# Order of the state-space products on TensorE: neighbours in different quarters of the array's columns

## The chip, the cores and the metric

The kernel runs on one core of a Trainium2 chip. The metric is the device time of one execution in microseconds, the median over several runs. The kernel before took 517.58 us (three runs, 512.52 to 519.69 us).

## What is computed

An encoder trunk of two layers over 256 tokens of 1024 channels, in float32. Each layer normalises its input, projects it into three branches, and projects the gated branches back. The first branch is a bidirectional state-space model: 32 groups of 16 channels drive a complex diagonal state of 64 numbers each.

```python
for l in range(DEPTH):
    h = rmsnorm(x, norm_g[l])
    xa, za, qb, kb, vb, zb, qc, kc, vc, zc = jnp.split(h @ w_in[l], split_points, axis=-1)
    ya = ssm_branch(xa, ...) * silu(za)       # state-space branch
    yb = na_branch(qb, kb, vb, ...) * silu(zb)       # neighbourhood attention, 8 heads
    yc = dilated_branch(qc, kc, vc, ...) * silu(zc)  # dilated attention, 8 heads
    x = x + concatenate([ya, yb, yc]) @ w_out[l]
return rmsnorm(x, final_g)

# ssm_branch, per direction: bu = b_bar u;  h = scan(lam_bar, bu);  y += Re(c h)
# then g = gelu(y), out = g * sigmoid(g @ glu_w + glu_b)
```

## The kernel before

The work of all stages is written as generators, each of which yields the engine and the buffers that its next step needs. A planner (`Flow.run`) with its own cost for each operation picks the next step by the earliest start and a rank, and so fixes, when the kernel is built, one order of instructions for each engine. `in_order` keeps that order. The planner's cost of a product depends on its shape and not on its neighbours. All weight and scratch transfers are issued by SyncE's queue (SP), in the planner's order too.

The big projections (`run_layer`, tile `pj`) take weights in pieces of 512 KB (`raw`). A piece is split into a high part `whi` (cast, ScalarE or VectorE) and a low part `wlo` (subtraction on VectorE), and TensorE forms three products. There are three buffers of `raw` and `whi` and two of `wlo`, so transfers, splitting and products move on together.

The state-space branch runs in chunks of T = 8 tokens, with four batches (`b`) of eight groups (`GB`) in each layer:

- `ssm_x` multiplies the chunked input `u` with the tables `wb` into the bank `psx`, and transposes into `E`, the chunk states.
- `ssm_scan` runs the recurrence over chunks on VectorE (`t1s`, `t2s`, `E`).
- `ssm_out` forms the tables `wc` on VectorE, two halves of four groups for each batch.
- `ssm_kernels` multiplies `bd` and `bs` (ScalarE copies) with `wc` and `cc` into the bank `psr`. Copies `rs`, by ScalarE and then VectorE, go through device memory (`rd`) and come back as `toep`, eight transfers for each batch.
- `ssm_y` copies `E` to `hy`, and adds three products per group in the bank `psy`: `u` with `toep`, and the two parts of `hy` with `wc`. The result goes on as `yt`, `ys`, `yd`, `yT` to the gate of the branch.

In `psx`, `psr` and `psy` the product of a group has 32 output rows, so it uses a quarter of the array's columns: `tile_position=(0, 32 * g4)` for group `g4` of a half `h`, with output in the 32 partitions from `32 * g4`. `psr` and `psy` take all products of a group in turn, and then the next group. `psx` has one product per group, and so goes from quarter to quarter. In a half, `psr` has for each group two products of T * CH = 128 columns and two of CH = 16 columns; `psy` has three of 128 columns.

Of the kernel before, what the change touches and what calls it, by code (L numbers as in the profile page):

```python
# [20 lines left out]
P = 128  # L21
# [8 lines left out]
CH = 16  # L30
T = 8
# [72 lines left out]
def ap(base, offset, dims):  # L104
    return bass.AP(base.tensor, base.offset + offset, dims)
# [8 lines left out]
class Event:  # L114
    t, eng = None, None
# [223 lines left out]
def trunk(ctx: ExitStack, tc: tile.TileContext, io):  # L339
    nc = tc.nc  # L340
    flow = Flow(tc)
    V, A, G, PE, SP = flow.V, flow.A, flow.G, flow.PE, flow.SP
# [5 lines left out]
    def new(tag, dims, dtype=F32, name=None):  # L348

        return sb.tile([P] + dims, dtype, name=name or tag, tag=tag, bufs=SLOTS[tag])  # L350

    def bank(tag, name=None):
        return psum.tile([P, 512], F32, name=name or tag, tag=tag, bufs=SLOTS[tag])

    def one(name, dims, dtype=F32, bufs=1):
        return sb.tile([P] + dims, dtype, name=name, tag=name, bufs=bufs)

    def dma(out, src):
        SP.dma_start(out, src)

    def copy(eng, out, src):
        if eng == "V":
            V.tensor_copy(out, src)
        else:
            A.copy(out, src)
# [45 lines left out]
    bd = one("bd", [2, GB, CH, 2])  # L411
# [50 lines left out]
    class Piece:  # L462
# [6 lines left out]
        def free(self):  # L469
            flow.free(*(("raw",) if self.plain else ("whi", "wlo")))  # L470
# [400 lines left out]
    def ssm_out(L, tb):  # L871

        for b in range(NB):
            wcs = []
            for h in range(2):
                g0 = b * GB + 4 * h
                yield "V", "g4", "tm", tb.ev, tb.wb_ev[2 * NB - 1]
                wc = new("g4", [2, 4, T, CH], name="wc")

                def qbc(t, i):  # L880
                    return free(t, i * T * GROUPS + g0, [[1, 4], [GROUPS, T], [0, CH]])

                def cbc(t, i):
                    return free(t, (i * GROUPS + g0) * CH, [[CH, 4], [0, T], [1, CH]])

                tm = new("tm", [4, T, CH], name="tmo")
                V.tensor_mul(tm, cbc(tb.csum, 0), qbc(tb.qc, 0))
                yield "V"
                V.tensor_mul(wc[:, 0], cbc(tb.cc, 1), qbc(tb.qsd, 0))
                yield "V"  # L890
                V.tensor_mul(wc[:, 1], cbc(tb.cc, 0), qbc(tb.qsd, 1))
                yield "V"
                V.tensor_sub(wc, free(tm, 0, [[0, 2], [1, 4 * T * CH]]), wc)
                flow.free("tm")
                wcs.append(wc)
            tb.wc.append(wcs)
            flow.set(tb.wc_ev[b])
            flow.spawn(ssm_kernels(L, b, tb, wcs), L.l)
            if b == NB - 1:
                flow.set(tb.wcs_ev)  # L900

    def ssm_kernels(L, b, tb, wcs):
        bb = tb.bb
        yield "A", "bd", "bs"
        bs = new("bs", [2, GB, CH, 2])
        for ri in range(2):
            src = free(bb, (ri * GROUPS + b * GB) * CH, [[1, GB * CH], [0, 2]])
            (A.copy if ri == 0 else lambda o, i: A.mul(o, i, -1.0))(bs[:, ri], src)
            yield "A"
        for d in range(2):  # L910
            r = slice(d * NST, (d + 1) * NST)
            A.copy(bd[r, :, :, :, d], bs[r, :, :, :, d])
            if d == 0:
                yield "A"
        yield "PE", "sm"
        ps = bank("sm", "psr")
        n = (T + 1) * CH
        for h in range(2):
            for g4 in range(4):
                g = 4 * h + g4  # L920
                o = ps[32 * g4:32 * g4 + 32, h * n:(h + 1) * n]
                for ri in range(2):
                    PE.matmul(o[:, :T * CH], lhsT=bd[:, ri, g].rearrange("p c d -> p (c d)"),
                              rhs=wcs[h][:, ri, g4].rearrange("p t c -> p (t c)"),
                              start=(h == 0 and ri == 0), stop=ri == 1, skip_group_check=True,
                              tile_position=(0, 32 * g4))
                for ri in range(2):
                    PE.matmul(o[:, T * CH:], lhsT=bs[:, ri, g].rearrange("p c d -> p (c d)"),
                              rhs=tb.cc[:, ri, b * GB + g], start=False, stop=ri == 1,
                              skip_group_check=True, tile_position=(0, 32 * g4))  # L930
        flow.free("bd", "bs")
        yield "A", "rs"
        rs = new("rs", [2, T + 1, CH])
        for h in range(2):
            A.copy(rs[:, h, :T, :], ps[:, h * n:h * n + T * CH].rearrange("p (t c) -> p t c", t=T))
        yield "V"
        for h in range(2):
            V.scalar_tensor_tensor(rs[:, h, T, :], eye16, tb.dsk[:, 2 * b + h:2 * b + h + 1],
                                   ps[:, h * n + T * CH:(h + 1) * n], ALU.mult, ALU.add)
        flow.free("sm")  # L940
        if b == NB - 1:
            flow.free("tab")
        yield "SP"
        rd = dram.tile([2, 4, CH, 15, CH], F32, name="rd", bufs=4)
        rdv = rd.rearrange("h g c t e -> (g c) h t e")
        dma(rdv[:, :, 0:7, :], rs[1::2, :, 1:T, :])
        dma(rdv[:, :, 7, :], rs[0::2, :, T, :])
        dma(rdv[:, :, 8:15, :], rs[0::2, :, 0:T - 1, :])
        flow.free("rs")
        flow.settle()  # L950

        tag = "toep" if b < TOEP else "qkv"
        yield ("SP", tag) if b < TOEP else ("SP", tag, L.br[1].v_ev[1])
        toep = new(tag, [GB, T * CH], name="toep")
        for g in range(GB):
            dma(toep[:, g, :], ap(rd, g * 15 * CH * CH, [[15 * CH, CH], [CH, T], [1, T * CH]]))
            if g % 2 and g < GB - 1:
                yield "SP"
        tb.toep[b] = toep
        flow.set(tb.toep_ev[b])  # L960

    def ssm_y(L, b, tb):
        gs = slice(b * GB, (b + 1) * GB)
        eng = yield "A/V", tb.scan_ev, tb.toep_ev[b], "hy"
        E = tb.E
        hy = new("hy", [2, GB, NCH])
        copy(eng, hy[:NST], E[:NST, :, gs, :NCH])
        eng = yield "A/V"
        copy(eng, hy[NST:], free(E[NST:], b * GB * N1 + NCH - 1, [[RS, 2], [N1, GB], [-1, NCH]]))
        yield "PE", "sm"  # L970
        wcs, u, toep = tb.wc[b], L.u[b], tb.toep[b]
        py = bank("sm", "psy")
        for h in range(2):
            for g4 in range(4):
                g = 4 * h + g4
                o = py[32 * g4:32 * g4 + 32, h * P:(h + 1) * P]
                PE.matmul(o, lhsT=u[:, g, :], rhs=toep[:, g, :], start=h == 0, stop=False,
                          skip_group_check=True, tile_position=(0, 32 * g4))
                for ri in range(2):
                    PE.matmul(o, lhsT=hy[:, ri, g, :], rhs=wcs[h][:, ri, g4].rearrange("p t c -> p (t c)"),  # L980
                              start=False, stop=ri == 1, skip_group_check=True, tile_position=(0, 32 * g4))
        flow.free("toep" if b < TOEP else "qkv", "g4", "g4", "u", "hy")
        tb.y_left -= 1
        if tb.y_left == 0:
            flow.free("E")
        yield "A", "yt"
        yt = new("yt", [2, P])
        A.copy(yt, py[:, :256].rearrange("p (h d) -> p h d", h=2))
        flow.free("sm")
        yield "PE", "sm"  # L990
        py2 = bank("sm", "psy2")
        for h in range(2):
            PE.transpose(py2[:, h * P:(h + 1) * P], yt[:, h, :], ident)
        flow.free("yt")
        yield "A", "ys"
        ys = new("ys", [GB, NCH])
        A.copy(ys, py2[:, :256].rearrange("p (g k) -> p g k", g=GB))
        flow.free("sm")
        yield "SP", L.yT.ask()
        yd = dram.tile([T, P, NCH], F32, name="yd")  # L1000
        dma(ap(yd, 0, [[S, P], [1, S]]), ys)
        flow.free("ys")
        flow.settle()
        yield "SP"
        dma(L.yT.tile[:, b, :].rearrange("p (t k) -> p t k", t=T), yd.rearrange("t c k -> c t k"))
        flow.set(L.y_ev[b])
# [665 lines left out]
```

## Time and profile before

| | |
|---|---|
| median of three runs | 517.58 us (512.52 to 519.69) |
| the profiled execution | 511.08 us, its span 509.3 us |
| busy share of the span: TensorE, weight loads, VectorE, ScalarE, GpSimd | 95%, 86%, 75%, 58%, 5% |
| granted TensorE clock, mean | 0.981 |
| mean share of the transfer engines' time, main queue | 70.1% |

A float32 product stands as two pairs of a weight load (PEld) and a product (PE) in the trace. The time of a product there is from its entry to its modelled end, so consecutive products overlap; the step from one start to the next is what it costs. Times are from the span's start.

### The profile page before, as it was taken

What the parts mean: (1) busy time and instruction counts of PE and PEld (TensorE: products, weight loads), DVE (VectorE), ACT (ScalarE), POOL (GpSimd) and SP (SyncE); (2) the same over time, 40 slices, a digit from 0 to 9 for tenths busy, and PEclk for the clock granted to TensorE, in tenths of its full rate; (3) what the DMA queues carried; (4) which work ended last, traced back from release to release, by engine and by line L of the source; (5) the groups of instructions that cost most, each with busy time, mean ns of one, the idle gap of its engine ahead of it and who ended that gap; (6) DMA issues with size and microseconds to landing.
All of it is one profiled execution on the core that took longest, in us unless ns stands there. A gap on an engine that the chain in (4) does not pass through costs nothing.

```text
span 509.3 us, 10599 instructions
## 1 busy us (share of the span) xinstructions
PE 483.6 (95%) x4076; PEld 436.0 (86%) x4076; DVE 381.3 (75%) x745; ACT 297.0 (58%) x596; POOL 24.6 (5%) x45
## 2 busy tenths in 40 slices
PE   8887988999999999989999699999999999999995
PEld 7676786698888999989998599998989799999995
DVE  5966767988997895457879678889788994358533
ACT  6432366566587665455545436767676776587432
POOL 1000102110000000000000010222000000000000
PEclk9988999999999999999999889999999999999999
DMA  7987798865663779874767997877565585664512
GB/s 261 299 236 247 218 258 232 222 172 166 140 143 106 219 260 278 245 215 162 252 205 211 262 268 204 186 170 178 136 126 134 138 261 182 184 167 168 187 41 84
DMA packets 73331, 99.61 MB, mean 196 GB/s; under 512 B 26768, under 2 KB 48400, under 8 KB 73280
## 3 DMA queue, kind: packets, MB, share of 16 engines
q1 hardware_dynamic: 73136, 98.83, 70.1%
q8 instruction: 32, 0.52, 0.4%
q14 instruction: 19, 0.16, 0.1%
q10 hardware_dynamic: 144, 0.10, 0.1%
HBM read 93.19 MB, written 5.72 MB: 194 GB/s over the span
## 4 chain that ended last, share of the span: by engine, by line
PE 67%; DMA 20%; DVE 6%; SPq 2%; ACT 2%; issue 2%; POOL 0%; DVEq 0%; POOLq 0%; ACTq 0%
PE pj L135 45%; PE psr L135 6%; PE sc L135 5%; DMA raw<-w_in 4%; DMA wb<-b_c 3%; DMA u<-xad 3%; PE po L135 3%; PE pp L135 3%; PE psy L135 3%; SPq L135 2%; DVE wb L135 2%; PE psx L135 2%; DMA qd<-qbt 2%; DMA raw<-w_out 1%; DMA xad<-xa 1%
## 5 line engine op out<-in xcount | busy, mean ns | idle before, releaser
L135 DVE TENSOR_TENSOR wlo<-raw,whi 128x1024 fp32r<-128x1024 f32 x92 | 113.6, 1234 | 55.6 <-PE pj L135 28.6
L135 ACT CAST whi<-raw 128x1024 fp32r<-128x1024 f32 x91 | 95.0, 1048 | 67.3 <-DMA raw<-w_in 28.2
L135 PE MATMUL pj<-h0h,whi 128*128 128x256 f32 x192 | 58.3, 304 | 0.0
L135 PE MATMUL pj<-h1h,whi 128*128 128x256 f32 x192 | 56.3, 293 | 0.0
L135 PE MATMUL pj<-h0h,wlo 128*128 128x256 f32 x192 | 55.1, 287 | 0.7 <-DVE wlo L135 0.7
L135 PE MATMUL pj<-h0l,whi 128*128 128x256 f32 x192 | 54.9, 286 | 0.0
L135 PE MATMUL pj<-h1h,wlo 128*128 128x256 f32 x192 | 53.9, 281 | 0.0
L135 PE MATMUL pj<-h1l,whi 128*128 128x256 f32 x192 | 53.9, 281 | 0.0
L135 PEld LDWEIGHTS pj<-h0h,whi 128*128 128x128 f32 x192 | 37.4, 195 | 5.7 <-issue 5.5
L135 PEld LDWEIGHTS pj<-h1h,whi 128*128 128x128 f32 x192 | 36.3, 189 | 2.7 <-issue 2.7
L135 PEld LDWEIGHTS pj<-h0h,wlo 128*128 128x128 f32 x192 | 37.3, 194 | 1.0 <-DVE wlo L135 0.9
L135 PEld LDWEIGHTS pj<-h0l,whi 128*128 128x128 f32 x192 | 37.3, 194 | 0.0
L135 PEld LDWEIGHTS pj<-h1h,wlo 128*128 128x128 f32 x192 | 36.2, 189 | 0.0
L135 PEld LDWEIGHTS pj<-h1l,whi 128*128 128x128 f32 x192 | 36.1, 188 | 0.0
L135 PE MATMUL pj<-xin,raw 128*128 128x256 f32 x128 | 32.5, 404 | 3.6 <-DMA raw<-w_in 2.8
L135 ACT ACTIVATE pt<-pt,sm 128x160 f32<-128x160 f32 (+1 forms) x63 | 28.3, 469 | 10.5 <-DVE sm L135 10.2
L135 PEld LDWEIGHTS pj<-xin,raw 128*128 128x128 f32 x128 | 24.5, 200 | 10.2 <-DVE xin L135 3.0
L135 PE MATMUL sc<-k,q 64*128 64x256 f32 (+1 forms) x128 | 31.0, 362 | 2.1 <-DVE nm L135 2.1
L135 ACT ACTIVATE pt<-pt,nm 128x160 f32<-128x160 f32 (+1 forms) x64 | 29.8, 468 | 5.3 <-DVE nm L135 5.1
L135 PE MATMUL psr<-wc,bd 128*32 128x128 f32 x256 | 31.1, 279 | 0.0
L135 POOL TENSOR_TENSOR bias<-bias,namask 128x320 f32<-128x320 f32 x16 | 19.5, 1220 | 222.8 <-DMA bias<-rpb 99.9
L135 PEld LDWEIGHTS sc<-k,q 64*128 64x128 f32 x128 | 19.8, 186 | 9.9 <-DVE nm L135 3.6
(198 smaller groups left out, 1300.5 us busy)
## 6 DMA issues: line engine op xcount, KB each, us to landing
raw<-w_in SPq DMA_DIRECT2D x78, 512.0 KB, 4.6
raw<-w_out SPq DMA_DIRECT2D x24, 512.0 KB, 3.4
wb<-b_c SPq DMA_DIRECT2D x32, 256.0 KB, 7.7
qrp<-qd SPq DMA_DIRECT2D x32, 256.0 KB, 5.0
bias<-vdram SPq DMA_DIRECT2D x16, 256.0 KB, 4.9
toep<-rd SPq DMA_DIRECT2D x64, 64.0 KB, 3.9
bias<-rpb SPq DMA_DIRECT2D x32, 116.0 KB, 5.5
raw<-glu_w SPq DMA_DIRECT2D x4, 512.0 KB, 4.0
```

The costliest lines, as they stand in the source:

```text
L135: return f(*args, **kw)
```

## The change

Two loops are turned inside out. In `ssm_kernels`, for each half, the first products of all four groups come first, then the second products of all four, and the same for the short products. In `ssm_y`, for each half, `u` with `toep` for four groups, then the first part of `hy` with `wc` for four groups, then the second. Operands, targets, number of products and the accumulation in each group's target stay.

```diff
@@ -915,17 +915,20 @@
         yield "PE", "sm"
         ps = bank("sm", "psr")
         n = (T + 1) * CH
+
         for h in range(2):
-            for g4 in range(4):
-                g = 4 * h + g4
-                o = ps[32 * g4:32 * g4 + 32, h * n:(h + 1) * n]
-                for ri in range(2):
-                    PE.matmul(o[:, :T * CH], lhsT=bd[:, ri, g].rearrange("p c d -> p (c d)"),
+            for ri in range(2):
+                for g4 in range(4):
+                    PE.matmul(ps[32 * g4:32 * g4 + 32, h * n:h * n + T * CH],
+                              lhsT=bd[:, ri, 4 * h + g4].rearrange("p c d -> p (c d)"),
                               rhs=wcs[h][:, ri, g4].rearrange("p t c -> p (t c)"),
                               start=(h == 0 and ri == 0), stop=ri == 1, skip_group_check=True,
                               tile_position=(0, 32 * g4))
-                for ri in range(2):
-                    PE.matmul(o[:, T * CH:], lhsT=bs[:, ri, g].rearrange("p c d -> p (c d)"),
+            for ri in range(2):
+                for g4 in range(4):
+                    g = 4 * h + g4
+                    PE.matmul(ps[32 * g4:32 * g4 + 32, h * n + T * CH:(h + 1) * n],
+                              lhsT=bs[:, ri, g].rearrange("p c d -> p (c d)"),
                               rhs=tb.cc[:, ri, b * GB + g], start=False, stop=ri == 1,
                               skip_group_check=True, tile_position=(0, 32 * g4))
         flow.free("bd", "bs")
@@ -971,14 +974,14 @@
         wcs, u, toep = tb.wc[b], L.u[b], tb.toep[b]
         py = bank("sm", "psy")
         for h in range(2):
-            for g4 in range(4):
-                g = 4 * h + g4
-                o = py[32 * g4:32 * g4 + 32, h * P:(h + 1) * P]
-                PE.matmul(o, lhsT=u[:, g, :], rhs=toep[:, g, :], start=h == 0, stop=False,
-                          skip_group_check=True, tile_position=(0, 32 * g4))
-                for ri in range(2):
-                    PE.matmul(o, lhsT=hy[:, ri, g, :], rhs=wcs[h][:, ri, g4].rearrange("p t c -> p (t c)"),
-                              start=False, stop=ri == 1, skip_group_check=True, tile_position=(0, 32 * g4))
+            for part in range(3):
+                for g4 in range(4):
+                    g = 4 * h + g4
+                    PE.matmul(py[32 * g4:32 * g4 + 32, h * P:(h + 1) * P],
+                              lhsT=u[:, g, :] if part == 0 else hy[:, part - 1, g, :],
+                              rhs=toep[:, g, :] if part == 0 else wcs[h][:, part - 1, g4].rearrange("p t c -> p (t c)"),
+                              start=h == 0 and part == 0, stop=part == 2, skip_group_check=True,
+                              tile_position=(0, 32 * g4))
         flow.free("toep" if b < TOEP else "qkv", "g4", "g4", "u", "hy")
         tb.y_left -= 1
         if tb.y_left == 0:
```

## Rows read from the trace of the kernel before

**Rows 1.** The page, the chain that ended last: shares of the span by line.
```profile
PE pj L135 45%; PE psr L135 6%; PE sc L135 5%; DMA raw<-w_in 4%; DMA wb<-b_c 3%; DMA u<-xad 3%; PE po L135 3%; PE pp L135 3%; PE psy L135 3%; SPq L135 2%; DVE wb L135 2%; PE psx L135 2%; DMA qd<-qbt 2%; DMA raw<-w_out 1%; DMA xad<-xa 1%
```
**Rows 2.** Busy time by stretch: start:end, us, busy us (instructions), granted clock, DMA share, GB/s.
```profile
105.00:176.00 71.00, 71.00 (x674) 62.78 (x674) 62.05 (x130) 48.85 (x113) 0.00 (x0) 1.00 0.60 157
176.00:226.00 50.00, 47.74 (x501) 45.35 (x497) 32.06 (x55) 25.14 (x40) 0.22 (x1) 1.00 0.85 246
...
324.60:388.00 63.40, 63.40 (x624) 56.13 (x623) 54.12 (x103) 42.25 (x107) 7.54 (x11) 1.00 0.71 158
...
423.40:446.00 22.60, 22.60 (x294) 21.41 (x294) 6.89 (x7) 11.57 (x21) 0.00 (x0) 1.00 0.65 181
```
**Rows 3.** Tile `psr`: ns min/median/max; first stage's stretch; its TensorE timeline (start, us).
```profile
L135 PE MATMUL psr<-wc,bd x256: 272/273/297, 105.1 to 387.2; 128*32 128x128 f32 x128
...
L135 PE MATMUL psr<-cc,bs x256: 179/183/183, 105.5 to 387.4; 128*32 128x16 f32 x128
...
105.06:109.01 3.95, 3.94 (x64) 3.90 (x64) 0.00 (x0) 0.00 (x0) 1.00 0.95 179
...
105.53 0.30 PE L135 MATMUL psr<-wc,bd 128*32 128x128 f32 x1
105.56 0.25 PE L135 MATMUL psr<-cc,bs 128*32 128x16 f32 x3
105.67 0.49 PE L135 MATMUL psr<-wc,bd 128*32 128x128 f32 x3
...
106.00 0.30 PE L135 MATMUL psr<-wc,bd 128*32 128x128 f32 x1
```
**Rows 4.** Tile `psy`, layer 1's first stage: its stretch, and its TensorE timeline.
```profile
423.38:425.90 2.52, 2.51 (x48) 2.31 (x48) 0.00 (x0) 1.00 0.84 255
...
423.63 0.27 PE L135 MATMUL psy<-wc,hy 128*32 128x128 f32 x1
423.64 0.30 PE L135 MATMUL psy<-toep,u 128*32 128x128 f32 x1
423.74 0.27 PE L135 MATMUL psy<-wc,hy 128*32 128x128 f32 x1
```
**Rows 5.** Tile `psx`, a half batch and a whole batch: busy PE, PEld, ACT.
```profile
98.37:98.95 0.58, 0.58 (x8) 0.16 (x8) 0.00 (x0) 1.00 0.99 396
278.47:279.48 1.01, 1.00 (x16) 0.42 (x16) 0.00 (x0) 1.00 0.57 109
...
L135 PEld LDWEIGHTS psx<-wb,u x128: 106/109/155, 58.0 to 369.6; 128*32 128x32 f32 x128
```
**Rows 6.** Waits (us in total, times, longest), 105 to 176, 324.6 to 388; VectorE's timeline.
```profile
DVE rs L135 <- ACT rs L135: 5.7, 4, 1.8
...
DVE rs L135 <- ACT rs L135: 5.5, 3, 2.0
...
388.23 0.42 DVE L135 CUSTOM_DVE_ANT_0 pt<-sc,bias 128x256 f32<-128x256 f32 x1 [1.24 <-PE pp L135]
```
**Rows 7.** Chain that ended last, 170 to 230 us: shares by line; pieces (start, us).
```profile
by line: DMA raw<-w_out 12.7%; SPq L135 12.5%; PE pj L135 11.5%; DMA toep<-rd 11.4%; DMA yd<-ys 9.0%; DMA yT<-yd 8.1%; DMA raw<-w_in 7.4%; PE psr L135 6.6%; PE psy L135 4.3%; issue 2.7%; ACT L135 2.1%; ACT hy L135 1.9%; DVE wlo L135 1.9%; A
...
175.96 0.37 DVE rs L135 x2
176.33 0.93 DVE t2s L135
```
**Rows 8.** Timelines: VectorE's second `wc` of layer 0, ScalarE's `hy` of layer 1.
```profile
100.15 1.22 DVE L135 TENSOR_TENSOR wc<-tmo,wc 128x1024 f32<-128x1024 f32 x1
...
422.21 0.63 ACT L135 COPY hy<-E 64x512 f32<-64x512 f32 x1
```
**Rows 9.** Stretches around a half clock, all work; last row `psx` alone. Clock third from last.
```profile
287.60:291.60 4.00, 0.00 (x0) 0.00 (x1) 3.30 (x4) 0.71 (x1) 0.50 (x1) 0.63 1.10 275
...
288.70:295.50 6.80, 3.87 (x21) 3.10 (x22) 3.16 (x4) 1.32 (x2) 0.00 (x0) 0.50 1.05 259
...
291.60:292.64 1.04, 1.01 (x8) 0.23 (x8) 0.00 (x0) 0.50 1.06 271
```

## The prediction

> **What bounds the kernel now.** I read the chain that ended last first. TensorE's big projections `pj` carry 45% of it; the chunk kernels `psr` are 6% of the span and the chunk outputs `psy` 3% [rows 1]. Then the busy time by stretch [rows 2]. From 105 to 176 us (layer 0) and from 324.6 to 388 us (layer 1), which hold four `psr` stages each, TensorE has no idle time, but VectorE has little: 71.00 − 62.05 = 8.95 us and 63.40 − 54.12 = 9.28 us. A gain of TensorE there runs into VectorE soon. From 176 to 226 us TensorE is 95% busy, yet the chain runs through VectorE, SyncE's queue and transfers [rows 7]; a gain of TensorE in that stretch is mostly turned into waiting. From 423.4 to 446 us (the four `psy` stages of layer 1) TensorE has no idle time and VectorE works 6.89 of 22.60 us: there TensorE alone sets the pace.
>
> **The present order, one stage.** A float32 product stands in the trace as two instructions, so a `psr` stage has 64 and a `psy` stage 48. In `psr`, eight instructions of one group write the same quarter before the next quarter's turn. Three of 128 columns last 0.49 us together, one alone 0.273 us: a step of (0.49 − 0.27)/2 = 0.109 us. Three of 16 columns last 0.25 us, one alone 0.183 us: a step of 0.03 us. A new group begins every 106.00 − 105.53 = 0.47 us [rows 3]: four steps of 0.109 us, with only the short products of the last group beside the next one's first. So the stage is serial, 8 × 0.47 us plus its end, and takes 3.93 us; all eight do. In `psy` the next group begins earlier: the first product of the second group starts at 423.64 us, between the third instruction (423.63) and the fourth (423.74) of the first, with three of that group still to start [rows 4]. The same holds in `psr`: the next group starts with the fifth of eight. I read both as a short queue in front of each quarter: what is listed next goes ahead as soon as no more than three instructions wait for the quarter before it. The stage then takes 2.51 us.
>
> **What the change costs.** It adds, removes and moves no instruction to another engine or queue; it permutes products within a stage, and the planner's cost for a stage is the same sum, so I take the order on every engine, the DMA issues too, as unchanged outside the stages. `psx` already has the wanted order, two instructions a quarter and then the next quarter. Sixteen of 256 columns take 1.00 us, eight take 0.58 us [rows 5]. Eight more cost 0.43 us, which is two steps of 0.215 us: four quarters run in the time of one. A stage is then two steps per eight instructions and 0.58 − 0.43 = 0.15 us of beginning and end.
> - `psr` after: a quarter has, in each half, four instructions of 0.109 us and four of 0.03 us. 2 × (0.436 + 0.12) + 0.15 = 1.26 us against 3.93 us: 2.67 us a stage, 21.4 us over eight.
> - `psy` after: 2 × 6 × 0.109 + 0.15 = 1.46 us against 2.51 us: 1.05 us a stage, 4.2 us over the four of layer 1, 4.2 us over those of layer 0.
> - New waits: the second half's `wc` is wanted some 1.3 us sooner in a stage. In the first stage it was ready at 100.15 + 1.22 = 101.37 us [rows 8] for a stage that starts at 105.06 us, so nothing waits. In `psy` four `toep` products now stand ahead of the first that reads `hy`, a small gain where `hy` comes last.
>
> The cost of a short product in four quarters at once is shown nowhere. Below lies zero (hidden), above a loading bound: the 16 weight loads of `psx` cover 0.42 us [rows 5], 0.026 us each, so 32 loads cost 0.84 us a stage against my 0.24 us. I keep 0.24 us, since two neighbours of `psx` run in less than a step; the other end makes `psr` 1.86 us, still 2.07 us better.
>
> **What of it reaches the end.** VectorE stands still in every `psr` stage, because the `rs` operation behind it is next in its order. It waits 5.7 us over the four stages of layer 0 and 5.5 us over three of layer 1; in the fourth stage of layer 1 it waits 1.24 us for `pp`, which follows `psr` on TensorE [rows 6]. No single wait is longer than 2.0 us, and the stage ends 2.67 us (or 2.07 us) sooner, so all eight vanish: 12.4 us. ScalarE's `rs` copy, which stands between the two, is set free by the same amount. What is late next is VectorE itself. The rest of its idle time in both stretches is 18.2 − 12.4 = 5.8 us; other pieces of it wait on TensorE and ScalarE. Bounds 0 and 5.8; I take 1.5 us, near the low end, because VectorE's order is fixed and no single wait there is large. That VectorE's gain, not TensorE's, is what arrives is seen at both exits: in layer 0 the chain goes on from `rs` to the scan's `t2s` on VectorE [rows 7], and in layer 1 the first `psy` at 423.38 us [rows 4] follows the `hy` copy that ended at 422.21 + 0.63 = 422.84 us [rows 8].
> From 423.4 us on the four `psy` count in full: 4.2 us (bounds 3 and 4.2, if a `toep` or weight comes later than its reader). In layer 0 the first `psy` is in the chain, the others are behind transfers: between 0 and 1.05 us, I take 0.5.
> Sum: 12.4 + 1.5 + 4.2 + 0.5 = 18.6 us. The profiled execution took 511.08 us (span 509.3), so it would become 492.5 us; the median of the runs is 517.58 us, 6.5 us above it, and I set the gain against that: 499.0 us.
>
> **Rivals.**
> - A, the forecast, VectorE limits: 12.4 to 23.4 us of gain with the bounds above, likely 15 to 23: 494 to 502 us. Chance 0.66.
> - B, all of TensorE's gain arrives in layers' `psr` stages: 21.4 + 4.2 + 0.5 = 26 us, 491.5 us. For it: TensorE is 100% busy there. Against it: 4 × 2.67 = 10.7 us is more than VectorE's whole idle time in either stretch. Chance 0.10.
> - C, the pair stays serial: the second instruction of a product blocks the next quarter until it starts. Then a quarter change helps once per pair: `psr` 16 × 0.112 + 16 × 0.033 + 0.15 = 2.5 us, 1.45 us less; VectorE's waits shrink by at most that, some 10.5 us; `psy` becomes 24 × 0.112 + 0.15 = 2.8 us, 0.3 us worse, 1.2 us in layer 1. Gain 9.3 us: 508.3 us. Against it: `psx` shows pairs that do not block. For it: `psx` has longer products and no accumulation into one place. Chance 0.13.
> - D, nothing changes: the loads of neighbouring quarters cannot overlap, and 64 loads of 0.110 us set the stage. Then 517.6 us. Against it: the 16 loads of `psx` of 0.109 us each would be 1.74 us and cover 0.42 us [rows 5]. [...] Chance 0.08.
> - E, slower: a faster TensorE waits more often, and its clock falls. After an idle stretch of 4.0 us the granted clock was 0.50 for 6.8 us, and eight instructions of `psx` took 1.01 us instead of 0.58 us [rows 9]. Half clock adds as much again as the work at full clock takes, 3.4 us per such stretch. Before, the two `psr` stretches ran at 1.00 [rows 2]. Only after 18.6/3.4 = 5.5 such stretches is the gain gone, and for over 2% slower there must be some 9 in 135 us. TensorE's new idle time there is about 10.7 − 6.5 = 4 us per stretch, in pieces of under a microsecond. 528 us or more; chance 0.03.
>
> **How the numbers follow.** The likeliest is A: 499.0 us. Leaving out the ends of B, all of E and most of D, the range is 490 to 509 us. Two per cent, about what a measurement of this kernel can tell from no change, is 10.4 us: below 507.2 us counts as faster. A and B lie below, and about half of C once run-to-run spread (512.52 to 519.69 us before) is counted: 0.66 + 0.10 + 0.07 = 0.83. Within 2%: the rest of C and D, 0.06 + 0.08, and a little of E, 0.15. Slower: 0.02.
>
> **What would show it.** In the profile after: `psr` stages of about 1.3 us and `psy` stages of about 1.5 us, with the sixteen or so starts of a row in four quarters within some 0.03 us; C would show 2.5 and 2.8 us. VectorE's wait for `rs` gone from the list of waits, VectorE over 93% busy in the stretches that now are 105 to 176 and 324.6 to 388 us, and TensorE idle there for the first time, waiting for VectorE's `wlo` or `nm`. The stretch of the layer 1 `psy` shorter by about 4 us. The forecast is wrong if `psr` shrinks and VectorE's busy share does not rise, or if the granted clock falls below 1.00 in those stretches.

## The result and the profile after

The changed kernel takes 496.39 us (median of four runs, 495.35 to 500.18) against 515.64 us of the kernel before (four runs): ratio 0.9636, 95% interval 0.9544 to 0.9727, so 19.25 us faster. The forecast was 499.0 us, a gain of 18.6 us, within a range of 490 to 509 us. The profiled execution took 496.33 us, its span 494.5 us.

The order of the instructions on VectorE, ScalarE, SyncE's queue and GpSimd is that of before, and on TensorE outside the two stages too. Busy time by stretch in the changed kernel, with the columns of [rows 2] (the busy times are those of TensorE, weight loads, VectorE, ScalarE and GpSimd): from the start of the first `psr` stage to the end of the last one in layer 0, the same in layer 1, the four `psy` stages of layer 1, and the rest.

```profile
107.05:167.75 60.70, 59.95 (x667) 51.51 (x667) 58.81 (x127) 47.69 (x111) 0.00 (x0) 1.00 0.64 163
317.28:372.86 55.58, 52.52 (x619) 44.94 (x618) 50.83 (x100) 41.58 (x104) 5.72 (x11) 1.00 0.74 169
409.39:424.97 15.58, 15.58 (x272) 14.38 (x271) 6.20 (x6) 10.63 (x19) 0.00 (x0) 1.00 0.73 209
424.97:494.50 69.53, 64.44 (x516) 64.11 (x512) 35.86 (x52) 35.41 (x52) 0.00 (x0) 0.90 0.42 130
```

The same stretches in the kernel before (here cut at the stages, in [rows 2] at round times):

```profile
105.07:175.38 70.31, 70.31 (x667) 62.30 (x666) 61.94 (x129) 48.34 (x111) 0.00 (x0) 1.00 0.60 155
324.63:387.54 62.91, 62.91 (x620) 55.66 (x619) 54.09 (x103) 41.86 (x104) 7.51 (x11) 1.00 0.71 158
423.39:443.23 19.84, 19.84 (x272) 18.65 (x271) 6.89 (x7) 10.83 (x19) 0.00 (x0) 1.00 0.63 175
443.23:509.30 66.07, 60.76 (x513) 60.19 (x512) 35.14 (x51) 35.37 (x51) 0.00 (x0) 0.98 0.43 133
```

The three stretches with the changed stages are 9.61, 7.33 and 4.26 us shorter, 21.2 us in all. VectorE's share rises to 58.81/60.70 = 97% in layer 0 and 50.83/55.58 = 91% in layer 1. Its busy time in these stretches falls by 3.1 and 3.3 us, partly because two and three of its instructions now lie outside them: the stretches are cut at TensorE's stages, and TensorE finishes further ahead of VectorE than before. TensorE, which had no idle time in the first two, has 0.75 and 3.06 us. The last stretch is 3.5 us longer at a lower clock; the experiments take that up.

One `psr` stage of the changed kernel on TensorE's timeline (start, length, form, count), to be set beside [rows 3]:

```profile
107.05 0.64 PE L135 MATMUL psr<-wc,bd 128*32 128x128 f32 x16
107.51 0.29 PE L135 MATMUL psr<-cc,bs 128*32 128x16 f32 x16
107.64 0.62 PE L135 MATMUL psr<-wc,bd 128*32 128x128 f32 x16
108.08 0.29 PE L135 MATMUL psr<-cc,bs 128*32 128x16 f32 x16
108.30 0.33 PE L135 MATMUL pp<-ident,pt 128*128 128x128 f32 x1
```

From 107.05 to 108.30 us it takes 1.25 us instead of 3.93. Its end is the start of the next product, at 108.30 us. The first sixteen instructions of 128 columns, four in each quarter, occupy 0.46 us (four start within 0.02 us, one in each quarter; the later steps from four to four are 0.11 us); in the old order the same sixteen were sixteen steps of 0.109 us, 1.74 us. One `psy` stage, beside [rows 4]:

```profile
409.39 0.43 PE L135 MATMUL psy<-toep,u 128*32 128x128 f32 x8
409.64 0.62 PE L135 MATMUL psy<-wc,hy 128*32 128x128 f32 x16
410.07 0.40 PE L135 MATMUL psy<-toep,u 128*32 128x128 f32 x8
410.29 0.62 PE L135 MATMUL psy<-wc,hy 128*32 128x128 f32 x16
410.84 0.39 PE L135 MATMUL pj<-h1h,whi 128*128 128x256 f32 x1
```

That is 1.45 us instead of 2.51. Behind the first `psr` stage, VectorE's timeline shows `rs` with no wait ahead of it, where it stood still for up to 2.0 us [rows 6]:

```profile
108.79 0.68 DVE L135 TENSOR_TENSOR wc<-cc,qsd 128x512 f32<-128x512 f32 x1
109.39 0.37 DVE L135 SCALAR_TENSOR_TENSOR rs<-eye,dsk,psr 128x16 f32<-128x16 f32 x2
```

What took its place in layer 1 stands in the list of waits from 317.28 to 372.86 us (us in total, times, longest):

```profile
POOL bias L135 <- DMA bias<-rpb: 12.0, 2, 8.5
...
DVE pt L135 <- POOL bias L135: 3.6, 1, 3.6
...
PE sc L135 <- DVE nm L135: 3.0, 2, 2.7
```

A bias for the attention heads comes late, GpSimd's sum on it is late, VectorE waits 3.6 us for that sum, and TensorE waits 2.7 us for VectorE's `nm`, with which the bank `sc` comes free. GpSimd's wait for the bias is the same in the kernel before (12.0 us, the longest 8.5), but there neither VectorE nor TensorE has a long wait behind it: they come to that place later, since each `psr` stage takes 2.7 us more. The last experiments test this.

In layer 0 the last `psy` stage starts and then stands still (TensorE's timeline; in brackets the wait):

```profile
199.61 0.43 PE L135 MATMUL psy<-toep,u 128*32 128x128 f32 x8
204.46 1.08 PE L135 MATMUL psy<-wc,hy 128*32 128x128 f32 x16 [4.42 <-ACT hy L135]
```

TensorE has done the four `toep` products and waits 4.42 us for the copy `hy`. ScalarE makes that copy from 203.17 us on, behind the cast of a piece of weights at 202.22 us, for which it waited 2.09 us for `raw<-w_out`. This is the gain of TensorE turned into waiting, as the forecast had it for 176 to 226 us of the kernel before.

### The profile page after: what moved, and what is told of

It reads as the page before. It is cut to its first block, busy times and chain, and to the rows that moved or that the text cites. A ratio compares the mean times of both kernels' runs of the same rounds, so it can differ in the third digit from the quotient of the medians.

```text
span 494.5 us, 10599 instructions
## 1 busy us (share of the span) xinstructions
PE 459.9 (93%) x4076; PEld 411.3 (83%) x4076; DVE 378.1 (76%) x745; ACT 296.3 (60%) x596; POOL 23.1 (5%) x45
## 4 chain that ended last, share of the span: by engine, by line
PE 56%; DMA 22%; DVE 12%; ACT 4%; issue 3%; SPq 2%; POOL 0%; DVEq 0%; POOLq 0%; ACTq 0%
PE pj L135 39%; DMA wb<-b_c 5%; PE sc L135 4%; DMA qrp<-qd 4%; DMA raw<-w_out 3%; DVE wlo L135 3%; DMA raw<-w_in 3%; PE po L135 2%; PE psy L135 2%; PE pp L135 2%; SPq L135 2%; PE warm L436 2%; DMA u<-xad 2%; DVE t1s L135 2%; DMA qd<-qbt 2%
## 5 line engine op out<-in xcount | busy, mean ns | idle before, releaser
L135 POOL TENSOR_TENSOR bias<-bias,namask 128x320 f32<-128x320 f32 x16 | 18.2, 1138 | 223.7 <-DMA bias<-rpb 100.3
L135 DVE TENSOR_TENSOR wb<-wb,qrp 128x1024 f32<-128x1024 f32 x16 | 20.0, 1250 | 5.3 <-DMA qrp<-qd 5.1
```

The costliest lines, as they stand in the source:

```text
L135: return f(*args, **kw)
```

## The experiments

The theory, as the author read it from [rows 3] to [rows 5]: the products of four quarters run in the time of one (eight more of `psx` cost 0.43 us, two steps), as long as the next one in the list finds a free place in the short queue of its quarter (at 423.64 us a new quarter starts with three instructions of the one before still to start); TensorE's gain then arrives up to what VectorE allows. The rivals name other limits; each run states its own.

**One stage at a time.** `psr_only` has the new loops in `ssm_kernels` alone, `psy_only` those in `ssm_y` alone; the diffs are the first and the second part of the change.

> Only the chunk kernels' stage (psr) has the new order; the outputs' stage (psy) keeps the old one. Theory (four quarters run at once, and the two stages add up): psr stages 1.25 us, psy stages 2.51 us as before, and the whole gain less about 4.5 us: 14 to 16 us faster than before, ratio about 0.97. Rival (the gain hangs on psy, where TensorE alone sets the pace, and VectorE takes back what psr gives): under 6 us faster.

> Only the outputs' stage (psy) has the new order. Theory: psy stages 1.45 us where nothing is late, psr stages 3.93 us; the four stages of layer 1 give 4.2 us, those of layer 0 between 0 and 1, so 4 to 5 us faster, ratio about 0.991. Rival (the gain hangs on psy): 13 us faster or more.

`psr_only`: 499.26 us, ratio 0.9714 (0.9639 to 0.9789). `psy_only`: 510.14 us, ratio 0.990 (0.9854 to 0.9946). The three stretches of each:

```profile
107.80:168.50 60.70, 59.99 (x667) 51.53 (x667) 58.76 (x126) 47.70 (x111) 0.00 (x0) 1.00 0.63 160
317.21:374.16 56.95, 53.90 (x619) 46.39 (x619) 50.67 (x100) 41.47 (x104) 6.96 (x11) 0.97 0.72 165
411.18:431.01 19.83, 19.83 (x271) 18.64 (x270) 6.64 (x7) 10.71 (x18) 0.00 (x0) 1.00 0.60 169
```

```profile
104.72:175.03 70.31, 70.31 (x667) 62.30 (x666) 61.66 (x129) 48.25 (x111) 0.00 (x0) 1.00 0.58 149
323.73:386.64 62.91, 62.91 (x620) 55.66 (x619) 54.12 (x103) 41.77 (x104) 7.78 (x11) 1.00 0.70 157
423.16:438.73 15.57, 15.57 (x271) 14.37 (x271) 5.86 (x6) 10.52 (x18) 0.00 (x0) 1.00 0.71 199
```

Each part moves its own stretches and leaves the others to the hundredth of a microsecond. 2.9% and 1.0% add up to 3.9%, against 3.6 to 3.7% for both; by the medians that is 14.6 us and 3.7 us, near the 14 to 16 and 4 to 5 us expected. In `psr_only` layer 1's stretch takes 56.95 us and not the 55.58 us of the changed kernel, at a granted clock of 0.97; the second profile of the changed kernel below has 56.83 us at 0.97, 3.4 us of it at half clock. The rival that the gain hangs on `psy` is out.

**Two quarters, and one.** `two_quarters` alternates between two quarters only, `same_quarter` takes both groups of a quarter in turn.

```diff
# two_quarters, against the changed kernel (in both stages)
-for h in range(2):
+for h, pair in ((0, (0, 1)), (0, (2, 3)), (1, (0, 1)), (1, (2, 3))):
...
-        for g4 in range(4):
+        for g4 in pair:
# same_quarter, against the kernel before (in both stages)
-for h in range(2):
-    for g4 in range(4):
+for g4 in range(4):
+    for h in range(2):
         g = 4 * h + g4
```

> In both stages the products alternate between two quarters only, then between the other two. With a short queue in front of each quarter (three instructions wait, one runs), the next two quarters start before the first two are through: psr 4 groups of about 0.46 us and an end, 2.1 us; psy 1.7 us; 14 to 17 us faster than before. Without a queue (two quarters at once, then the next two): psr 4 x 0.556 + 0.15 = 2.4 us, psy 4 x 0.654 + 0.15 = 2.8 us, so psy slower than before and the whole some 9 us faster.

> The opposite of the change: both groups of a quarter in turn, then the next quarter. With the queue of three the next quarter starts with the fourth last instruction: psr 3 x 1.0 + 1.11 + 0.15 = 4.25 us instead of 3.93, psy 3 x 0.9 + 1.33 + 0.15 = 4.2 us instead of 2.51; eight times 0.3 and four times 1.7 us make the whole 9 us slower than before, ratio 1.017. Rival (a stage is bound by the number of its instructions or loads, and the order of quarters changes nothing but at single places): psr 3.9, psy 2.5, the time as before.

`two_quarters`: 499.16 us, ratio 0.972 (0.965 to 0.9789). Its first `psr` stage, and its first `psy` stage of layer 1:

```profile
103.58:105.68 2.10, 2.10 (x64) 2.06 (x64) 0.00 (x0) 0.00 (x0) 1.00 0.93 222
...
408.80:410.49 1.69, 1.69 (x48) 1.49 (x48) 0.00 (x0) 1.00 0.56 196
```

`same_quarter`: 525.55 us, ratio 1.0269 (1.0216 to 1.0322), slower. The same two stages:

```profile
105.56:109.89 4.33, 4.33 (x64) 4.29 (x64) 0.00 (x0) 0.00 (x0) 1.00 0.87 191
...
428.47:432.61 4.14, 4.14 (x48) 3.94 (x48) 0.00 (x0) 1.00 0.74 237
```

The queue of three foretold 2.1 and 1.7 us, 4.25 and 4.2 us; measured are 2.10 and 1.69, 4.33 and 4.14 us. By the medians the whole is 14.7 us faster (14 to 17 expected) and 11.7 us slower (9 expected). Two quarters at a time without a queue would have been 2.4 and 2.8 us. So the order of the same products alone makes a `psy` stage 4.14, 2.51, 1.69 or 1.45 us, and the kernel between 2.7% slower and 3.7% faster.

One more rival can be settled here: that products wait because they add into the same target, and not because they use the same quarter. In `same_quarter` the six instructions for one group's target are followed by six for another target in the same quarter (TensorE's timeline of that `psy` stage):

```profile
428.71 0.60 PE L135 MATMUL psy<-wc,hy 128*32 128x128 f32 x4
429.15 0.38 PE L135 MATMUL psy<-toep,u 128*32 128x128 f32 x2
429.37 0.27 PE L135 MATMUL psy<-wc,hy 128*32 128x128 f32 x1
429.38 0.30 PE L135 MATMUL psy<-toep,u 128*32 128x128 f32 x1
429.48 0.27 PE L135 MATMUL psy<-wc,hy 128*32 128x128 f32 x1
```

The new target begins at 429.15 us, four steps of 0.109 us behind 428.71 us: it does not start early. The next quarter does, at 429.38 us, with three instructions of the quarter before it still to start. So it is the quarter that counts. The depth of three can be held against others by an estimate of the author's, from steps of 0.109 us in a quarter, starts some 0.007 us apart in different quarters (as the 429.37 and 429.38 us above) and 0.15 us of end: a queue of two would make the old `psy` stage 3.1 us and a queue of four 1.8 us, where a queue of three gives 2.4 us and 2.51 us were measured.

**Less work for VectorE.** `light_before` and `light_after` leave out two of four operations on `wc`, in the old and in the new order.

```diff
-                V.tensor_mul(tm, cbc(tb.csum, 0), qbc(tb.qc, 0))
+                flow.charge("V", "tensor_mul", (tm, cbc(tb.csum, 0), qbc(tb.qc, 0)), {})
...
-                V.tensor_sub(wc, free(tm, 0, [[0, 2], [1, 4 * T * CH]]), wc)
+                flow.charge("V", "tensor_sub", (wc, wc, wc), {})
```

> The old order of products, and VectorE leaves out two of the four operations that form wc (the product tmo and the final subtraction, 16 x (0.68 + 1.22) us; the tables hold other numbers). The planner is charged for them as before, so the order on every engine stays. From the start of the first psr stage to the end of the last one a layer takes 70.3 and 62.9 us in the kernel before. Theory (there TensorE alone sets the pace): 70.3 and 62.9 us again, within 0.5; the whole 0 to 4 us faster, from stretches where VectorE leads. Rival (VectorE sets the pace before already): both stretches some 6 us shorter.

> The new order of products, with the same two VectorE operations left out. In the changed kernel the two stretches take 60.7 and 55.6 us. Theory (VectorE takes back a part of what TensorE gains): without its work TensorE's whole gain of 4 x 2.68 us arrives, 70.3 - 10.7 = 59.6 and 62.9 - 10.7 = 52.2 us, so about 1 us and 3.5 us less than in the changed kernel. Rival (what is missing to the whole gain is lost to transfers or to GpSimd's bias sums): 60.7 and 55.6 us again.

`light_before`: 512.91 us, ratio 0.998 (0.9933 to 1.0028), no change. `light_after`: 490.24 us, ratio 0.9553 (0.9495 to 0.9611). The two `psr` stretches of `light_before`, then of `light_after`:

```profile
107.66:177.97 70.31, 70.31 (x667) 62.32 (x667) 52.51 (x117) 48.30 (x111) 0.00 (x0) 1.00 0.56 149
327.45:390.36 62.91, 62.91 (x620) 55.66 (x619) 44.65 (x93) 41.67 (x104) 4.90 (x10) 1.00 0.69 158
```

```profile
106.12:166.39 60.27, 59.97 (x667) 51.54 (x666) 50.19 (x115) 47.62 (x111) 0.00 (x0) 1.00 0.61 159
314.56:368.00 53.44, 52.26 (x620) 44.95 (x619) 42.18 (x90) 41.28 (x104) 6.35 (x11) 1.00 0.75 176
```

In the old order some 9.4 us less of VectorE's work in each stretch changes nothing: TensorE alone sets the pace there, so VectorE's waits behind `psr` were not what made these stretches long. In the new order it is worth 60.70 − 60.27 = 0.43 us in layer 0 and 55.58 − 53.44 = 2.14 us in layer 1. What is missing to TensorE's whole gain (59.6 and 52.2 us) was 1.1 and 3.4 us, so VectorE's load accounts for 0.4 and 2.1 us of it, and 0.7 and 1.3 us lie elsewhere. In layer 1 that share is not VectorE's alone: an experiment below wins 1.7 us there by moving the bias transfers, and 2.1 and 1.7 us together are more than 3.4 us. They are two ways out of one wait.

**Both kernels once more.** No edit.

> The changed kernel once more, for a second profile and times beside the others. Ratio 0.96 to 0.97 to the kernel before. If the 16 us at half clock at the end of its first profile come from the change, they stand here too and not in a second profile of the kernel before; if they fall at random on either kernel, the second profile of the kernel before can show them too.

> The kernel before once more, one profile. If the clock falls at the end by itself, the stretch from the end of the last psy stage to the end of the span takes 69 to 70 us at a clock below 0.9 in its last part, as in the changed kernel, instead of the 66.1 us of the first profile; if the change causes it, 66 us at full clock.

The changed kernel: 494.55 us, ratio 0.9627 (0.9588 to 0.9666). The kernel before, one execution: 516.24 us. The stretch behind the last `psy` stage, in the second profile of the changed kernel and then of the kernel before:

```profile
424.49:492.86 68.37, 63.50 (x516) 63.29 (x512) 35.85 (x52) 35.52 (x52) 0.00 (x0) 0.93 0.41 131
```

```profile
445.44:514.46 69.02, 64.16 (x513) 63.85 (x512) 35.16 (x51) 35.44 (x51) 0.00 (x0) 0.90 0.41 128
```

The long stretch at the end stands in the old order too: 69.02 us at a granted clock of 0.90, as against 66.07 us at 0.98 in the first profile. So the change does not make it. It is also part of why the first two profiles differ by 14.8 us of span only, and the medians by 19.25 us: the first profile of before was lucky by about 3 us at its end.

**The new wait in layer 1.** `bias_pool` has the transfers for the bias issued by GpSimd, `bias3` gives the biases a third buffer.

```diff
# bias_pool, against the changed kernel
-                        dma(t[:, qt, :n], ap(io["rpb"], ...))
+                        flow.charge("SP", "dma_start", (t[:, qt, :n], src), {})
+                        nc.gpsimd.dma_start(t[:, qt, :n], src)
# bias3, against the changed kernel
-SLOTS = dict(..., bias=2, ...)
+SLOTS = dict(..., bias=3, ...)
```

> The changed kernel, with the 32 transfers bias<-rpb issued by GpSimd's queue, just ahead of the sums that read them, instead of by SyncE's; the planner is charged as before, so the order elsewhere stays. In the changed kernel TensorE waits in layer 1 for sc, 2.7 us at once, behind VectorE's nm, GpSimd's bias sum and bias<-rpb, which stands behind toep<-rd in SyncE's queue. Theory (that queue makes the new wait): the wait of 2.7 us goes, layer 1's stretch of psr stages takes 52.5 to 54.5 us instead of 55.6 and 56.8, the whole 1 to 3 us faster than the changed kernel, ratio 0.957 to 0.961. Rival (VectorE alone limits it): 55.6 us again and the same time. It can also turn slower, if GpSimd issues its transfers later than SyncE did.

> The changed kernel with three buffers for the attention biases instead of two, so that a bias is asked for one head earlier; the planner sees it and may move orders. Theory (the late bias makes the new wait of 2.7 us in layer 1): that wait goes, 1 to 3 us faster than the changed kernel. Rival: the same time.

`bias_pool`: 495.68 us, ratio 0.9628 (0.959 to 0.9666). `bias3`: 494.1 us, ratio 0.9596 (0.9552 to 0.964). The two `psr` stretches of `bias_pool`:

```profile
107.89:169.63 61.74, 60.40 (x667) 51.55 (x666) 60.12 (x130) 47.56 (x110) 0.00 (x0) 1.00 0.62 159
318.18:372.08 53.90, 52.54 (x620) 44.93 (x619) 50.26 (x100) 41.58 (x104) 11.75 (x19) 1.00 0.79 182
```

`bias_pool` shortens layer 1's stretch by 1.7 us (2.9 us against the second profile, which had a piece at half clock), as the theory had it, and TensorE's longest wait for `sc` there falls from 2.7 to 1.3 us. So the rival, that VectorE alone limits this stretch, falls. But layer 0's stretch grows by 1.0 us and the whole stays as it was, against the 1 to 3 us expected: the place of the wait is shown, a gain is not. In `bias3` the planner moved work between the stretches, so here is the time from layer 1's first `psr` stage to its first `psy` stage, in `bias3` and then in the changed kernel:

```profile
318.22:405.48 87.26, 86.43 (x869) 73.53 (x868) 83.55 (x178) 66.85 (x161) 6.45 (x10) 1.00 0.68 178
```

```profile
317.28:409.39 92.11, 88.35 (x887) 75.85 (x886) 86.04 (x181) 70.00 (x164) 5.72 (x11) 1.00 0.71 175
```

TensorE's idle time falls from 3.76 to 0.83 us. That fits a late bias, but the orders moved too, so `bias_pool` is the cleaner evidence. In the whole little of it is left: the interval overlaps with that of the changed kernel in `both`, and the profile has 2.0 us more between layer 0's last `psy` stage and layer 1's first `psr` stage (112.1 us against 110.1). Whether `bias3` is faster than the change stays open.

**A plan nearer to the measured stages.**

```diff
# replanned, against the changed kernel, in Flow.charge
                 elif m <= 32:
-                    cost = (cost + 3 * 0.027) / 4
+                    cost = cost / 4
```

> The changed kernel, with the planner's cost of a product in a quarter set to a fourth of the cost of the whole, without the 81 ns that it adds: a psr stage is then planned at 1.1 us instead of 1.8 us (measured 1.25), a psy stage at 1.3 us instead of 1.8 (measured 1.45). All orders may move. Theory (a plan nearer to the measured times follows the gain): 0 to 4 us faster than the changed kernel. Rival (ranks and patience were fitted to the old cost): some us slower.

497.88 us, ratio 0.9681 (0.9635 to 0.9727): not the 0 to 4 us gain of the theory over the changed kernel, although its plan is nearer to the stages as measured. The rival, that the planner's other settings were fitted to the old cost, is not excluded and was not tested further. No version beat the changed kernel beyond its interval.

## Why the prediction was right, point by point

- **The old stages are serial within a quarter, with a queue of three behind it.** Right. Three other orders gave the stage times that this reading foretells, within 0.1 us. Loads of different quarters overlap here: with all 128 rows in each product, 64 loads and products pass in 1.25 us, where 64 loads of 0.110 us one after another would take 7 us, more than the old stage's 3.93 us too. And products do not always start in the order of the list: in `same_quarter` the product that starts at 429.38 us is listed behind the one that starts at 429.48 us.
- **The new stages.** 1.26 and 1.46 us were worked out from `psx` [rows 5]; the eight `psr` stages take 1.25 to 1.27 us, and the `psy` stages that do not wait take 1.45 us. The short products cost what one alone costs, 0.03 us a step in each quarter (sixteen of them, four in each, from 107.51 to 107.64 us); the loading bound that would have made it 1.86 us did not come. Rivals C and D are out.
- **VectorE's waits vanish, 12.4 us.** Right: no wait of VectorE for `rs` is left.
- **The rest of VectorE's idle time, 1.5 us.** The size is right, in part by luck. The forecast counts VectorE's time, so the stretch has to be cut at VectorE's instructions: from `wlo` (layer 0) or `tmo` (layer 1) ahead of the first `rs` to the end of the last `rs`, in the kernel before and then in the changed one.

```profile
105.40:176.33 70.93, 70.93 (x673) 62.46 (x671) 61.98 (x132) 48.45 (x112) 0.00 (x0) 1.00 0.60 156
325.44:388.95 63.51, 63.51 (x621) 56.26 (x620) 54.00 (x107) 42.51 (x107) 6.70 (x11) 1.00 0.70 157
```

```profile
107.05:170.15 63.10, 62.35 (x686) 53.38 (x686) 61.18 (x132) 49.07 (x115) 0.00 (x0) 1.00 0.65 168
318.62:375.63 57.01, 53.95 (x578) 46.40 (x579) 52.22 (x107) 43.11 (x108) 5.43 (x9) 1.00 0.74 169
```

  The two became 7.83 and 6.50 us shorter, 14.3 us in all (13.4 us in the second profile), where the forecast had 12.4 + 1.5 = 13.9 us. Its 1.5 us came out as 1.9 us, but from pieces that it did not have: VectorE's idle time beside the 12.4 us fell by about 3 us more, its busy time for the same instructions fell by 2.6 us (why stays open), and the new wait for the bias cost 3.6 us. In layer 0 VectorE went from 87% busy to 97%: a busy share of 87% on an engine beside one at 100% says little about how far it can be pushed.
- **VectorE is late next.** Right in layer 1, and there only together with the late bias: VectorE's load accounts for 2.1 of the 3.4 us that are missing. In layer 0 it accounts for 0.4 us, and TensorE comes within 1.1 us of its whole gain; that is nearer to rival B than to the forecast, which had VectorE set the limit in both. The bias that comes late through transfers and GpSimd was not in the forecast. The share of 93% that VectorE was to pass was reached in layer 0 (97%) and not in layer 1 (91%); in `bias_pool` it is 50.26/53.90 = 93% there.
- **`psy` of layer 1, 4.2 us.** 19.84 − 15.58 = 4.26 us.
- **`psy` of layer 0, 0.5 us.** No gain clear of the spread between two profiles. From the last `psr` stage to the last `psy` stage of layer 0 the kernel before takes 36.3 us and the changed one 39.4 us, because TensorE comes early and waits for `hy`. Most of this is TensorE's lead running out: between VectorE's marks, from the last `rs` of layer 0 to `tmo` in layer 1, it is 149.1 us before and 148.5 us after (149.7 us in the second profile).
- **The sum.** At VectorE's marks the terms that the profiles show are 14.33 + 0.64 + 4.26 us, and 0.68 us between the last `rs` and the first `psy` of layer 1 (34.44 us before, 33.76 after): 19.9 us. In the second profile they are 13.41 − 0.63 + 4.27 + 0.07 = 17.1 us. Forecast 18.6, measured 19.25 and 18.04 us. So the terms hold one by one, within about 1 us each, although TensorE and not VectorE set the pace of the old stretches. The lower end of A was too low by its own bounds: 12.4 + 0 + 3 + 0 is 15.4 us and not 12.4 us.
- **Rival E, the clock.** A half clock behind a wait is there on a small scale. In the second profile of the changed kernel the granted clock of layer 1's stretch is 0.97, below the 1.00 that the prediction named as a sign of being wrong. TensorE does nothing there from 333.20 to 335.90 us, waiting for `sc` (the forecast had its new idle time in pieces of under a microsecond), and soon after runs at half clock:

```profile
337.20:340.60 3.40, 3.40 (x18) 3.40 (x17) 2.89 (x5) 0.91 (x2) 0.88 (x1) 0.50 0.97 267
333.20:335.90 2.70, 0.01 (x1) 0.00 (x0) 1.73 (x6) 0.99 (x3) 1.05 (x2) 1.00 0.89 113
```

  That stretch took 56.83 us there and 55.58 us in the first profile, which has the same wait and no fall. So 3.4 us at half clock cost about 1.3 us here, where the forecast took 3.4 us for 6.8 us, and do not come every time; at this price it would take 14 of them to lose the gain. That half clock doubles the time of the work itself is nearly what the first profile shows: `pj` products of 128 columns start 0.11 us apart at 476 us, at a clock of 1.00, and 0.21 us apart at 482 us, at 0.50. In the first profile the clock is 0.50 behind the wait of 4.42 us in layer 0's last `psy` stage, which is part of why the rest of that stage takes 2.7 us, where a whole stage at 1.00 takes 1.45 us:

```profile
204.00:207.40 3.40, 2.94 (x41) 2.41 (x42) 2.49 (x5) 0.82 (x2) 0.21 (x1) 0.50 0.75 248
```

  The kernel before has such a piece too, 6.8 us at 0.50 [rows 9], and up to the end of the last `psy` stage the mean granted clock is 0.98 in the first profile of either kernel. So no net loss from the clock is seen there.

## What to carry to other kernels

Where small products share the array by columns, as these of 32 columns do, list them so that neighbours stand in different quarters: the same 48 instructions took 1.45 us in that order, 2.51 us with one group after the other, and 4.14 us with both groups of a quarter in turn. By the reading that fits these runs, a product listed behind its own quarter's backlog holds up all that follow. A stage of the same kernel that already has the wanted order gives the price of the change to the hundredth of a microsecond. What then arrives at the end is decided by who set the pace and who is late next: here TensorE alone had set the pace of the `psr` stretches, and its gain arrived up to the 0.75 and 3.06 us in which it now waits for others.

## What the runs showed of the hardware that was not expected

- The stage times of three new orders agree within 0.1 us with one rule that fits the old order too: TensorE behaves as if in front of each quarter of the columns three instructions could wait while one runs, and as if the list stopped at the first that finds no place (`psr` 1.26, 2.1 and 4.25 us foretold, 1.25 to 1.27, 2.10 and 4.33 us measured; `psy` 1.46, 1.7 and 4.2 us foretold, 1.45, 1.69 and 4.14 us measured; the old `psy` 2.4 us estimated, 2.51 us measured). No row of a trace shows such a queue itself; the rule is an inference from start times. The depth was read off two boundaries of the old order; that it holds for three other orders was not to be expected.
- The granted clock falls to half near the end of the span in the first profile of the changed kernel, at 480.5 us, while TensorE is busy, and a low clock there is seen in both orders. Behind the last `psy` stage its mean is 0.89 to 0.93 in both profiles of the changed kernel, the second of before, `light_before` and `bias_pool`, and the stretch takes 68.2 to 69.8 us; in `light_after` and the first profile of before the mean is 0.98, and it takes 66.0 and 66.1 us. In the changed kernel, before and after the fall:

```profile
470.00:480.50 10.50, 10.50 (x93) 10.50 (x93) 3.02 (x4) 3.38 (x7) 0.00 (x0) 1.00 0.01 2
480.50:494.50 14.00, 8.91 (x42) 8.61 (x41) 4.28 (x13) 2.32 (x7) 0.00 (x0) 0.50 0.26 76
```

  What sets it off there was not tried.
